# Two PSUM tiles of four banks and seven-product weights prepared a pair ahead, in a hybrid decoder layer on Trainium2

## The chip, the cores and the metric

The kernel runs on one core of one Trainium2 chip. The metric is the device time of one execution in microseconds, the median of several runs. TensorE (PE in the profile) does the matmuls, VectorE (DVE), ScalarE (ACT) and GpSimd (POOL) the rest; the SP queue issues the weight transfers.

## The reference

One layer on a sequence of 256 tokens, width 2048, float32:

```python
u = rmsnorm(h)                    # [q | k | v | z | xBC | dt | gates] = u @ w_in
A = sliding_window_sink_attention(q, k, v, sinks) @ w_attn_br
B = (rmsnorm(ssd(conv(xBC), dt) * silu(z))) @ w_ssd_br
h += (sigmoid(gate_attn) * A + sigmoid(gate_ssd) * B) @ w_o
h += (silu(rmsnorm(h) @ w_gate) * (rmsnorm(h) @ w_up)) @ w_down     # FFN 5632
h += sigmoid(rmsnorm(h) @ w_ple_gate) * (p @ w_ple_proj)
out = rmsnorm(h)
```

## The kernel before

**Products.** Every operand is split into a high part `wh` (a cast by ScalarE) and a low part `wl` (a subtraction by VectorE), and a product is three matmuls: high by high, high by low, low by high. Activations lie in SBUF transposed as such pairs (128 features by 256 tokens); weights stream from memory in transfers of 512 KB on the SP queue, through pools `wraw`, `whi`, `wlo` of 8 KB (per partition) buffers.

**Two kinds of block.** `nblock` computes 512 columns for two blocks of 128 tokens in two PSUM accumulators; the projections of the first part, attention and the SSD mixer (to about 520 us) and the per-layer embedding (from about 1480 us) use it. `wide_block` (L280) computes two column blocks by two token blocks, with the K tiles in pairs `kp`. A plain pair is 24 matmuls for each of its two halves `q`. A pair in `forms` is done with seven products in place of eight: its weights are the raw blocks b11, b21, b22 and four sums of blocks, t1 to t4 (`tr`, L328), each split again into `th` and `tl` (L336, L337), and the token side has its own sums (`token_forms`). Four of the seven go into four `shared` accumulators of the other bank group; `mid` (L352 to L355) combines these after the last formed pair, and `settle` (L360) adds them to the four main accumulators. There are 23 wide blocks (2 gates, 2 for `w_ssd_br`, 2 for `w_o`, 11 hidden, 6 for `w_down`) with 40 formed pairs; 17 of the blocks have two of them.

**PSUM.** Two pools, `acc` and `aux`, with four buffers each; every buffer is a tile of its own, one bank of 128 x 512. `psum.reverse()` swaps the groups at each wide block, so the next block's accumulators aren't those that the last block still settles.

**The side queue.** Work that isn't a product (transposes, token forms, sums of squares) waits in `side`, and `pump(n)` lets n items out between groups of matmuls. `transpose_pair` (L150) is four transposes into one bank, then `split_to`: ScalarE's cast (L132) and VectorE's subtraction (L133). For a hidden block, `settle`, ScalarE's silu (L1046) and VectorE's multiplication (L1047) come first, and two such flips of its result follow among the matmuls of the next block. In attention `p_flip` transposes the probabilities in 24 steps: two transposes (L904), a cast (L908), a subtraction (L909).

**Order.** Each engine works through its instructions in a fixed order, which the framework's scheduler makes when the kernel is built; it also places the waits, from the reads and writes of tiles.

Of the kernel before, what the change touches and what calls it, by code (L numbers as in the profile page):

```python
# [18 lines left out]
P = 128  # L19
# [4 lines left out]
NB = 512  # L24
# [37 lines left out]
def block_kernel(ctx: ExitStack, tc: tile.TileContext, x, x_t, p_t, positions, vecs, rows, g_final,  # L62
# [11 lines left out]
    acc_p = ctx.enter_context(tc.tile_pool(name="acc", bufs=4, space=bass.MemoryType.PSUM))  # L74
    aux_p = ctx.enter_context(tc.tile_pool(name="aux", bufs=4, space=bass.MemoryType.PSUM))
# [8 lines left out]
    psum = [(acc_p, "acc"), (aux_p, "aux")]  # L84

    def acc_tile():
        pool, name = psum[0]
        return pool.tile([P, NB], F32, name=name, tag=name)

    def aux_tile():  # L90
        pool, name = psum[1]
        return pool.tile([P, NB], F32, name=name, tag=name)
# [145 lines left out]
    class Sums:  # L238


        def __init__(self, tile_of, products):
            self.tile, self.left, self.first = tile_of(), 3 * products, True
# [37 lines left out]
    def wide_block(halves, lhs, nk, forms, pumps=1):  # L280
# [9 lines left out]
        c11, c12, c21, c22 = sums = [  # L290
            Sums(acc_tile, 2 * (np_ - ns) + (ns if i < 3 else 0)) for i in range(4)]
        shared, done = None, 0
        parts = [None] * 4

        def load(q, kp, dst):
            w, col0 = halves[q]
            nc.sync.dma_start(out=dst, in_=w[2 * kp * P:2 * (kp + 1) * P, col0:col0 + NB].rearrange(
                "(k p) n -> p k n", p=P))

        for kp in range(np_):  # L300
            ev, od = lhs(2 * kp), lhs(2 * kp + 1)
            tok = [[[x[:, t * P:(t + 1) * P] for x in k] for k in (ev, od)] for t in range(NT)]
            if kp not in forms:
                for q in range(2):
                    wr = wraw_p.tile([P, 2, NB], F32, name="wr", tag="wr")
                    load(q, kp, wr)
# [7 lines left out]
                    pump(pumps)  # L314
                continue
            if shared is None:
                shared = [Sums(aux_tile, ns) for _ in range(4)]
            q1, q5, q6, q7 = shared
            a, g2, f3, s3 = [[forms[kp][:, i, 0], forms[kp][:, i, 1]] for i in range(4)]
            raw = [wraw_p.tile([P, 2, NB], F32, name="wr", tag="wr") for _ in range(2)]  # L320
            for q in range(2):
                load(q, kp, raw[q])
            tr = big([P, 4, NB], F32, name="tr")
            for o, x, y in ((tr[:, 0], raw[0][:, 0], raw[1][:, 0]),
                            (tr[:, 1], raw[1][:, 0], raw[1][:, 1]),
                            (tr[:, 2], tr[:, 1], raw[0][:, 0]),
                            (tr[:, 3], tr[:, 2], raw[0][:, 1])):
                nc.vector.tensor_tensor(out=o, in0=x, in1=y, op=ALU.add)  # L328
            split = []
            for x, xh, xl in (  # L330
                    (raw[0], whi_p.tile([P, 2, NB], F32R, name="wh", tag="wh"),
                     wlo_p.tile([P, 2, NB], F32R, name="wl", tag="wl")),
                    (raw[1][:, 1:2], whi_p.tile([P, 2, NB], F32R, name="wh", tag="wh")[:, 1:2],
                     wlo_p.tile([P, 2, NB], F32R, name="wl", tag="wl")[:, 1:2]),
                    (tr, big([P, 4, NB], F32R, name="th"), big([P, 4, NB], F32R, name="tl"))):
                nc.scalar.copy(out=xh, in_=x)  # L336
                nc.vector.tensor_tensor(out=xl, in0=x, in1=xh.bitcast(F32), op=ALU.subtract)  # L337
                split.extend((xh[:, i], xl[:, i]) for i in range(x.shape[1]))
            b11, b21, b22, t1, t3, t2, t4 = split
# [3 lines left out]
            q6.add(g2, t2)  # L343
            q7.add(s3, t3)
            q5.add(a, t1)
            c21.add(tok[1][1], t4)
            pump(2 * pumps)
            done += 1
            if done == ns:
                mid = big([P, 4, NB], F32, name="mid")  # L350
                parts = [mid[:, i] for i in range(4)]
                nc.scalar.copy(out=parts[0], in_=q1.tile)  # L352
# [3 lines left out]
        return [x.tile for x in sums], parts  # L356

    def settle(i, sums, parts, out=None):
# [4 lines left out]
    def add_settled(i, dst, sums, parts):  # L363
        nc.vector.tensor_tensor(out=dst, in0=dst, in1=parts[i],
                                op=ALU.subtract if i % 2 else ALU.add)
        nc.vector.tensor_tensor(out=dst, in0=sums[i], in1=dst, op=ALU.add)
# [623 lines left out]

    gates = []
    for jj in range(2):
        sums, parts = wide_block(column_pair(w_in, GSO, jj), lhs_u, KD, uforms)
        for i in range(4):
            settle(i, sums, parts)
            nc.scalar.activation(out=parts[i], in_=parts[i], func=AF.Sigmoid,
                                 scale=r1[:, i // 2:i // 2 + 1])
        gates.append(parts)
    mforms = form_tiles((5,), "mforms")
    for jj in range(2):  # L1000
        sums, parts = wide_block(column_pair(w_ssd_br, 0, jj), lambda k: stat(yT, k), KD, yforms)
        for i in range(4):
            t, c = i // 2, cols(2 * jj + i % 2)
            settle(i, sums, parts)
            nc.vector.scalar_tensor_tensor(out=parts[i], in0=parts[i], scalar=r2[:, t:t + 1],
                                           in1=gates[jj][i], op0=ALU.mult, op1=ALU.mult)
            nc.vector.tensor_tensor(out=merged[t][:, c], in0=merged[t][:, c], in1=parts[i],
                                    op=ALU.add)
        for q in range(2):
            queue_flip(merged, mergedT, 2 * jj + q, None, mforms)  # L1010
# [14 lines left out]
    def add_to_h(jj, sums, parts):  # L1025
        for i in range(4):
            add_settled(i, h[i // 2][:, cols(2 * jj + i % 2)], sums, parts)

    ssq3 = mean_parts(4, EPS, "ssq3")
    for jj in range(2):  # L1030
        add_to_h(jj, *wide_block(column_pair(w_o, 0, jj), lambda k: stat(mergedT, k), KD, mforms))
        for q in range(2):
            queue_flip(h, hT, 2 * jj + q, V_GFFN, hforms)
            side.append(lambda j=2 * jj + q: square_sum(j, ssq3))
# [4 lines left out]
    def hidden(j, dst, kp0, forms):  # L1039
        sums, parts = wide_block(((w_gate, j * NB), (w_up, j * NB)), lambda k: stat(hT, k), KD,  # L1040
                                 hforms)
        act = [roll("act") for _ in range(NT)]
        for i in range(4):
            settle(i, sums, parts, None if i % 2 else act[i // 2])
# [12 lines left out]
    for j0, j1, apairs in thirds:  # L1057
# [13 lines left out]
        for jj in range(2):  # L1071
            add_to_h(jj, *wide_block(column_pair(w_down[j0 * NB:j1 * NB], 0, jj),
                                     lambda k, a=actT: stat(a, k), 4 * (j1 - j0), aforms))
            if last:
                for q in range(2):
                    queue_flip(h, h2T, 2 * jj + q, V_GPLE)
                    side.append(lambda j=2 * jj + q: square_sum(j, ssq4))
# [174 lines left out]
```

## Time and profile before

| | before |
|---|---|
| median of 3 runs | 1595.94 us (1594.6 to 1597.67) |
| profiled execution, its own time | 1596.97 us |
| its span, first to last instruction | 1595.3 us |
| TensorE busy | 1574.4 us, 99% |
| VectorE busy | 1200.7 us, 75% |
| ScalarE busy | 845.1 us, 53% |
| mean granted clock of TensorE | 0.997 |

Busy shares are those of the whole span. Idle time of an engine counts for the total only if it lies on the chain of work that ends last. In groups by line, the columns are busy us and mean ns of one instruction, then idle us just before them.

### The profile page before, as it was taken

The numbers are of one execution on the slowest core, as the hardware profiler recorded it, in microseconds if no ns is written. First come the engines' busy times: TensorE is split into PE (matmuls) and PEld (weight loads), VectorE is DVE, ScalarE is ACT, GpSimd is POOL, SyncE is SP. The second block draws the span as 40 slices with busy tenths as digits, with TensorE's granted clock in tenths as the row PEclk, the third lists the DMA queues.
The fourth block names the chain that finished last, engine by engine and source line by source line (L and its number), as shares of the span: only waits on it lengthen the run. The fifth ranks groups of instructions, "written<-read, shape, count | busy, mean of one in ns | idle before, by whom it ended". The sixth has DMA issues, their size and how long they took to land.

```text
span 1595.3 us, 19976 instructions
## 1 busy us (share of the span) xinstructions
PE 1574.4 (99%) x7294; PEld 1300.2 (82%) x7294; DVE 1200.7 (75%) x1507; ACT 845.1 (53%) x1073; POOL 132.1 (8%) x136
## 2 busy tenths in 40 slices
PE   9999999999999999999999999999999999999997
PEld 7988888888888888788788888788888878888886
DVE  7676767666666768788888887887877788788764
ACT  6654665555644544455655554455545444556543
POOL 1014224143210000000000000000000000000000
PEclk9999999999999999999999999999999999999999
DMA  8566435555646666665566655566665566755662
GB/s 268 175 195 183 142 105 158 159 159 158 177 158 182 210 200 212 208 195 188 175 202 191 198 193 190 185 211 194 193 195 173 196 207 195 225 188 182 197 217 100
DMA packets 152562, 296.63 MB, mean 186 GB/s; under 512 B 9536, under 2 KB 9664, under 8 KB 152080
## 3 DMA queue, kind: packets, MB, share of 16 engines
q1 hardware_dynamic: 151168, 290.76, 58.2%
q0 software_dynamic: 576, 3.47, 0.7%
q8 instruction: 57, 0.93, 0.2%
q10 hardware_dynamic: 720, 1.14, 0.2%
q14 instruction: 41, 0.34, 0.1%
HBM read 293.23 MB, written 2.10 MB: 185 GB/s over the span
## 4 chain that ended last, share of the span: by engine, by line
PE 93%; DMA 2%; DVE 2%; ACT 2%; issue 1%; POOL 0%; POOLq 0%; DVEq 0%; ACTq 0%
PE aux L248 30%; PE acc L248 27%; PE acc L204 9%; PE acc L205 9%; PE acc L206 9%; PE aux L150 1%; DMA wr<-in_w_down_dram 1%; DMA wr<-in_w_ple_gate_dram 1%; PE aux L739 1%; PE acc L150 1%; PE aux L920 1%; PE acc L233 0%; PE aux L233 0%; PE aux L234 0%; PE aux L235 0%
## 5 line engine op out<-in xcount | busy, mean ns | idle before, releaser
L308 ACT CAST wh<-wr 128x1024 fp32r<-128x1024 f32 x280 | 293.8, 1053 | 266.3 <-PE aux L248 91.6
L310 DVE TENSOR_TENSOR wl<-wr,wh 128x1024 fp32r<-128x1024 f32 x280 | 337.1, 1220 | 86.7 <-issue 37.3
L195 DVE TENSOR_TENSOR wl<-wr,wh 128x1024 fp32r<-128x1024 f32 (+1 forms) x172 | 227.6, 1330 | 122.0 <-PE acc L205 92.0
L193 ACT CAST wh<-wr 128x1024 fp32r<-128x1024 f32 (+1 forms) x172 | 173.8, 1013 | 170.9 <-PE acc L206 135.5
L248 PE MATMUL aux<-wh,flipT 128*128 128x512 f32 x736 | 237.6, 392 | 0.0
L248 PE MATMUL acc<-wh,flipT 128*128 128x512 f32 x640 | 208.3, 392 | 0.0
L204 PE MATMUL acc<-wh,uT 128*128 128x512 f32 (+1 forms) x512 | 200.2, 391 | 0.9 <-ACT cb L466 0.9
L206 PE MATMUL acc<-wh,uT 128*128 128x512 f32 (+1 forms) x512 | 194.0, 379 | 0.0
L205 PE MATMUL acc<-wl,uT 128*128 128x512 f32 (+1 forms) x512 | 193.8, 379 | 0.0
L248 PEld LDWEIGHTS aux<-wh,flipT 128*128 128x128 f32 x736 | 138.1, 188 | 28.3
L248 PE MATMUL aux<-wl,flipT 128*128 128x512 f32 x368 | 143.8, 391 | 0.5 <-DVE wl L310 0.5
L336 ACT CAST wh<-wr 128x1024 fp32r<-128x1024 f32 x80 | 66.8, 837 | 140.7 <-PE aux L248 64.0
L248 PEld LDWEIGHTS acc<-wh,flipT 128*128 128x128 f32 x640 | 120.2, 188 | 24.8 <-ACT wh L336 0.2
L248 PE MATMUL acc<-wl,flipT 128*128 128x512 f32 x320 | 124.6, 389 | 0.0
L204 PEld LDWEIGHTS acc<-wh,uT 128*128 128x128 f32 x512 | 96.3, 188 | 18.4 <-issue 1.4
L205 PEld LDWEIGHTS acc<-wl,uT 128*128 128x128 f32 x512 | 96.3, 188 | 17.6 <-issue 1.0
L337 DVE TENSOR_TENSOR tl<-tr,th 128x2048 fp32r<-128x2048 f32 x40 | 91.7, 2291 | 25.2 <-ACT th L336 25.2
L206 PEld LDWEIGHTS acc<-wh,uT 128*128 128x128 f32 x512 | 96.1, 188 | 17.8
L336 ACT CAST th<-tr 128x2048 fp32r<-128x2048 f32 x40 | 76.5, 1912 | 55.2 <-DVE tr L328 55.0
L248 PE MATMUL aux<-wh,actT 128*128 128x512 f32 x292 | 95.3, 393 | 0.0
L248 PE MATMUL acc<-wh,actT 128*128 128x512 f32 x292 | 93.5, 390 | 0.0
L328 DVE TENSOR_TENSOR tr<-wr 128x512 f32<-128x512 f32 x80 | 52.8, 686 | 40.3 <-DMA wr<-in_w_down_dram 21.7
(476 smaller groups left out, 2764.5 us busy)
## 6 DMA issues: line engine op xcount, KB each, us to landing
wr<-in_w_in_dram SPq DMA_DIRECT2D x144, 512.0 KB, 3.7
wr<-in_w_gate_dram SPq DMA_DIRECT2D x88, 512.0 KB, 3.8
wr<-in_w_up_dram SPq DMA_DIRECT2D x88, 512.0 KB, 4.4
wr<-in_w_down_dram SPq DMA_DIRECT2D x88, 512.0 KB, 4.4
wr<-in_w_ssd_br_dram SPq DMA_DIRECT2D x32, 512.0 KB, 4.8
wr<-in_w_o_dram SPq DMA_DIRECT2D x32, 512.0 KB, 4.2
wr<-in_w_ple_gate_dram SPq DMA_DIRECT2D x32, 512.0 KB, 4.6
wr<-in_w_in_dram SPq DMA_DIRECT2D x32, 256.0 KB, 4.2
```

The costliest lines, as they stand in the source:

```text
L150: nc.tensor.transpose(out=ps[:, j, t * P:(t + 1) * P], in_=src[t][:, c:c + P], identity=ident)
L193: nc.scalar.copy(out=wh, in_=wr)
L195: nc.vector.tensor_tensor(out=wl, in0=wr, in1=wh.bitcast(F32), op=ALU.subtract)
L204: nc.tensor.matmul(o, hi[:, ts], wh[:, kk, cs], start=(k == 0), stop=False)
L205: nc.tensor.matmul(o, hi[:, ts], wl[:, kk, cs], start=False, stop=False)
L206: nc.tensor.matmul(o, lo[:, ts], wh[:, kk, cs], start=False, stop=(k == nk - 1))
L248: nc.tensor.matmul(self.tile, a, b, start=self.first, stop=self.left == 0)
L308: nc.scalar.copy(out=wh, in_=wr)
L310: nc.vector.tensor_tensor(out=wl, in0=wr, in1=wh.bitcast(F32), op=ALU.subtract)
L328: nc.vector.tensor_tensor(out=o, in0=x, in1=y, op=ALU.add)
L336: nc.scalar.copy(out=xh, in_=x)
L337: nc.vector.tensor_tensor(out=xl, in0=x, in1=xh.bitcast(F32), op=ALU.subtract)
```

## The change

PSUM becomes two tiles of four banks (`Banks`, a ring of four through `take`), so that one VectorE operation can cover two banks: settling is 2 operations of 2 x 512 per block in place of 4 of 512, `mid` takes 3 VectorE operations in place of 4, and what follows (gates, merge, the addition to h) goes over 1024 columns. A formed pair's raw weights lie in one 8 KB tile `raw` and are prepared by the generator `prepared` in three steps beside the pair in front: the two transfers; the sums (one operation of 1024, two of 512) and the casts; the subtractions. Nothing is pumped while `shared` is in use, and otherwise `pump(min(2 * kp + q, 2))`; the sums of squares of h are queued behind both flips. Matmuls and transposes are as many as before. The diff, cut:

```diff
-    acc_p = ctx.enter_context(tc.tile_pool(name="acc", bufs=4, space=bass.MemoryType.PSUM))
-    aux_p = ctx.enter_context(tc.tile_pool(name="aux", bufs=4, space=bass.MemoryType.PSUM))
+    psum_p = ctx.enter_context(tc.tile_pool(name="psum", bufs=1, space=bass.MemoryType.PSUM))
+    class Banks:
+        def __init__(self, name):
+            self.all, self.next, self.held = psum_p.tile([P, 4, NB], F32, name=name), 0, False
+        def take(self):
+            assert not self.held
+            self.next = (self.next + 1) % 4
+            return self.all[:, (self.next - 1) % 4]
+    psum = [Banks("acc"), Banks("aux")]
...
-    def wide_block(halves, lhs, nk, forms, pumps=1):
+    def wide_block(halves, lhs, nk, forms):
...
-        c11, c12, c21, c22 = sums = [
-            Sums(acc_tile, 2 * (np_ - ns) + (ns if i < 3 else 0)) for i in range(4)]
+        mine, other = psum
+        c11, c12, c21, c22 = [
+            Sums(mine.all[:, i], 2 * (np_ - ns) + (ns if i < 3 else 0)) for i in range(4)]
...
+        def prepared(kp):
+            raw = big([P, 4, NB], F32, name="raw")
+            nc.sync.dma_start(out=raw[:, 0:4:3], in_=block(1, kp))
+            nc.sync.dma_start(out=raw[:, 1:3], in_=block(0, kp))
+            yield
+            tr = big([P, 4, NB], F32, name="tr")
+            th = big([P, 4, NB], F32R, name="th")
+            nc.vector.tensor_tensor(out=tr[:, 0:2], in0=raw[:, 1:4:2],
+                                    in1=raw[:, 0:1].broadcast_to([P, 2, NB]), op=ALU.add)
+            for i in (2, 3):
+                nc.vector.tensor_tensor(out=tr[:, i], in0=tr[:, i - 1], in1=raw[:, i - 1],
+                                        op=ALU.add)
+            wh = [whi_p.tile([P, 2, NB], F32R, name="wh", tag="wh") for _ in range(2)]
+            nc.scalar.copy(out=wh[0], in_=raw[:, 1:3])
+            nc.scalar.copy(out=wh[1][:, 0], in_=raw[:, 3])
+            nc.scalar.copy(out=th, in_=tr)
+            yield
+            wl = [wlo_p.tile([P, 2, NB], F32R, name="wl", tag="wl") for _ in range(2)]
+            tl = big([P, 4, NB], F32R, name="tl")
+            for x, xh, xl in ((raw[:, 1:3], wh[0], wl[0]), (raw[:, 3], wh[1][:, 0], wl[1][:, 0]),
+                              (tr, th, tl)):
+                nc.vector.tensor_tensor(out=xl, in0=x, in1=xh.bitcast(F32), op=ALU.subtract)
+            yield
...
             if kp not in forms:
+                step(kp + 1)
                 for q in range(2):
...
-                    pump(pumps)
+                    step(kp + 1)
+                    if shared is None or mid is not None:
+                        pump(min(2 * kp + q, 2))
                 continue
             if shared is None:
-                shared = [Sums(aux_tile, ns) for _ in range(4)]
+                shared = [Sums(other.all[:, i], ns) for i in range(4)]
+                other.held = True
...
-            pump(2 * pumps)
...
-                for o, x, y, op in ((3, 0, q6, ALU.subtract), (2, 3, q7, ALU.add),
-                                    (1, 3, q5, ALU.add), (3, 2, q5, ALU.add)):
-                    nc.vector.tensor_tensor(out=parts[o], in0=parts[x], in1=y.tile, op=op)
...
+                nc.vector.tensor_tensor(out=mid[:, 3], in0=mid[:, 0], in1=q6.tile,
+                                        op=ALU.subtract)
+                nc.vector.tensor_tensor(out=mid[:, 1:3],
+                                        in0=mid[:, 3:4].broadcast_to([P, 2, NB]),
+                                        in1=other.all[:, 1:3], op=ALU.add)
+                nc.vector.tensor_tensor(out=mid[:, 3], in0=mid[:, 2], in1=q5.tile, op=ALU.add)
+                other.held = False
...
-        nc.vector.tensor_tensor(out=parts[i] if out is None else out, in0=sums[i], in1=parts[i],
-                                op=ALU.subtract if i % 2 else ALU.add)
...
+        for i, op in enumerate((ALU.add, ALU.subtract)):
+            nc.vector.tensor_tensor(out=mid[:, i:4:2], in0=mine.all[:, i:4:2], in1=mid[:, i:4:2],
+                                    op=op)
+        return mid
```

How the order moves. First TensorE's order at a hidden block's join, around the second flip of the finished hidden block (`act<-` or `mid<-` is what is transposed, `flipT` the tokens of the block that runs). A wait is named by its semaphore: DVE_49 is VectorE's, Activation_49 ScalarE's. Before:

```order
3230 L248 MATMUL acc<-wl,flipT 128x512
3231 L248 MATMUL acc<-wh,flipT 128x512
3232 L150 MATMUL aux<-ident,act 128x128 x4
3233 L248 MATMUL acc<-wh,flipT 128x512 [waits Activation_49]
3234 L248 MATMUL acc<-wl,flipT 128x512
3235 L248 MATMUL acc<-wh,flipT 128x512 x2
3236 L248 MATMUL acc<-wl,flipT 128x512
3237 L248 MATMUL acc<-wh,flipT 128x512 x2
3238 L248 MATMUL acc<-wl,flipT 128x512
```

And of the change at the same place (L157 are the transposes, L255 the products):

```order
3227 L255 MATMUL acc<-wl,flipT 128x512
3228 L255 MATMUL acc<-wh,flipT 128x512
3229 L157 MATMUL aux<-ident,mid 128x128 [waits DVE_49]
3230 L157 MATMUL aux<-ident,mid 128x128 x3
3231 L255 MATMUL aux<-wh,flipT 128x512 [waits DVE_49,Activation_49]
3232 L255 MATMUL acc<-wh,flipT 128x512 [waits Activation_49]
3233 L255 MATMUL acc<-wl,flipT 128x512 [waits DVE_49]
3234 L255 MATMUL acc<-wh,flipT 128x512 x2
3235 L255 MATMUL acc<-wl,flipT 128x512
```

The transposes and the two matmuls behind them now stand behind waits for VectorE and ScalarE, and one of the matmuls writes into the group that the flip uses (`aux`). ScalarE's order there, before (L132 is the flip's cast, L308 and L336 weight casts):

```order
517 L1046 ACTIVATE act<-act,r_6432 128x512 [waits Pool_49]
518 L1046 ACTIVATE act<-act,r_6432 128x512 [waits DVE_49]
519 L308 CAST wh<-wr 128x1024 [waits DMAHW4_49,PE_49,Activation_49]
520 L336 CAST wh<-wr 128x1024 [waits DMAHW5_49,PE_49,Activation_49]
521 L132 CAST actT<-aux 128x512 [waits PE_49]
522 L336 CAST wh<-wr 128x512 [waits DMAHW6_49,PE_49,Activation_49]
523 L132 CAST actT<-aux 128x512 [waits PE_49]
524 L308 CAST wh<-wr 128x1024 [waits DMAHW7_49,DVE_49,PE_49]
525 L336 CAST th<-tr 128x2048 [waits DVE_49]
526 L308 CAST wh<-wr 128x1024 [waits DMAHW0_49,PE_49,Activation_49]
```

And of the change (L139 is the flip's cast, L321 to L323 cast a formed pair's weights, L351 a plain pair's):

```order
536 L1069 ACTIVATE mid<-mid,r_6160 128x512 [waits Pool_49]
537 L1069 ACTIVATE mid<-mid,r_6160 128x512
538 L139 CAST actT<-aux 128x512 [waits DVE_49,PE_49] x2
539 L321 CAST wh<-raw 128x1024 [waits DMAHW1_49]
540 L322 CAST wh<-raw 128x512 [waits DMAHW0_49,Activation_49]
541 L351 CAST wh<-wr 128x1024 [waits DMAHW4_49,Activation_49]
542 L351 CAST wh<-wr 128x1024 [waits DMAHW5_49,Activation_49]
543 L323 CAST th<-tr 128x2048 [waits DVE_49]
```

The two flips' casts stand side by side now, and three weight casts follow them that stood partly ahead of them. Last, TensorE's order at the probability flips (L904 before, L927 in the change). Before:

```order
883 L904 MATMUL aux<-ident,sc 128x128 [waits DVE_49,Pool_49]
884 L904 MATMUL aux<-ident,sc 128x128
885 L204 MATMUL acc<-wh,uT 128x512 [waits Activation_49]
886 L904 MATMUL aux<-ident,sc 128x128 [waits DVE_49,Pool_49]
887 L904 MATMUL aux<-ident,sc 128x128
888 L904 MATMUL aux<-ident,sc 128x128 [waits Activation_49]
889 L904 MATMUL aux<-ident,sc 128x128
890 L205 MATMUL acc<-wl,uT 128x512
891 L904 MATMUL aux<-ident,sc 128x128 [waits Activation_49]
892 L904 MATMUL aux<-ident,sc 128x128
893 L206 MATMUL acc<-wh,uT 128x512
894 L204 MATMUL acc<-wh,uT 128x512
```

And of the change:

```order
924 L927 MATMUL aux<-ident,sc 128x128 [waits DVE_49,Pool_49]
925 L927 MATMUL aux<-ident,sc 128x128
926 L927 MATMUL aux<-ident,sc 128x128 [waits DVE_49]
927 L927 MATMUL aux<-ident,sc 128x128
928 L927 MATMUL aux<-ident,sc 128x128 [waits DVE_49]
929 L927 MATMUL aux<-ident,sc 128x128
930 L927 MATMUL aux<-ident,sc 128x128 [waits DVE_49]
931 L927 MATMUL aux<-ident,sc 128x128
932 L927 MATMUL aux<-ident,sc 128x128 [waits DVE_49]
933 L927 MATMUL aux<-ident,sc 128x128
```

Projection matmuls (L204 to L206) stood between the pairs of transposes; now five pairs follow one another, each behind a wait for VectorE.

## Rows read from the trace of the kernel before

**Rows 1.** The page: span, busy time of the engines, the chain by engine.
```profile
span 1595.3 us, 19976 instructions
...
PE 1574.4 (99%) x7294; PEld 1300.2 (82%) x7294; DVE 1200.7 (75%) x1507; ACT 845.1 (53%) x1073; POOL 132.1 (8%) x136
...
PE 93%; DMA 2%; DVE 2%; ACT 2%; issue 1%; POOL 0%; POOLq 0%; DVEq 0%; ACTq 0%
```

**Rows 2.** Windows by stage: length, busy us (instructions) of PE, PEld, DVE, ACT, POOL; clock; DMA.
```profile
0.00:520.00 520.00, 515.07 (x2519) 430.47 (x2520) 357.19 (x527) 294.84 (x444) 125.92 (x128) 1.00 0.58 171
520.00:1480.00 960.00, 954.42 (x4264) 781.59 (x4263) 770.97 (x889) 494.36 (x547) 3.88 (x5) 1.00 0.61 196
1480.00:1596.00 116.00, 104.94 (x514) 88.10 (x512) 72.55 (x93) 55.94 (x82) 2.30 (x3) 0.97 0.50 165
```

**Rows 3.** What TensorE waited for: us in total, times, longest.
```profile
PE acc L248 <- DVE wl L337: 3.6, 3, 1.5
...
PE acc L204 <- ACT cb L466: 0.9, 1, 0.9
```

**Rows 4.** The chain of waits, one step in a wide block: start, us.
```profile
662.55 11.56 PE acc L248 x51
```

**Rows 5.** Timeline of a hidden block's join: start, us, engine, line.
```profile
814.75 0.60 PE L150 MATMUL aux<-ident,act 128*128 128x128 f32 x4
...
815.10 0.48 PE L248 MATMUL acc<-wh,flipT 128*128 128x512 f32 x1
...
815.51 0.58 ACT L132 CAST actT<-aux 128x512 fp32r<-128x512 f32 x1
...
816.13 0.69 DVE L133 TENSOR_TENSOR actT<-aux,actT 128x512 fp32r<-128x512 f32 x1
```

**Rows 6.** Groups by line, wide blocks: busy, mean ns of one; idle before.
```profile
L337 DVE TENSOR_TENSOR tl<-tr,th 128x2048 fp32r<-128x2048 f32 x40 | 91.7, 2291 | 25.2 <-ACT th L336 25.2
...
L336 ACT CAST th<-tr 128x2048 fp32r<-128x2048 f32 x40 | 76.5, 1912 | 55.2 <-DVE tr L328 55.0
...
L328 DVE TENSOR_TENSOR tr<-tr,wr 128x512 f32<-128x512 f32 x80 | 55.1, 688 | 1.6
...
L337 DVE TENSOR_TENSOR wl<-wr,wh 128x1024 fp32r<-128x1024 f32 x40 | 48.8, 1219 | 2.0 <-PE aux L248 1.1 <-issue 0.9
...
L336 ACT CAST wh<-wr 128x1024 fp32r<-128x1024 f32 x40 | 42.2, 1054 | 90.8 <-PE aux L248 42.6 <-PE acc L248 34.7 <-DMA wr<-in_w_down_dram 11.6
...
L336 ACT CAST wh<-wr 128x512 fp32r<-128x512 f32 x40 | 24.8, 620 | 49.9 <-PE aux L248 21.4 <-PE acc L248 20.6 <-DVE wl L337 5.9
...
L1046 ACT ACTIVATE act<-act,r 128x512 f32<-128x512 f32 x22 | 15.8, 722 | 1.0
...
L1047 DVE SCALAR_TENSOR_TENSOR act<-mid,r,act 128x512 f32<-128x512 f32 x22 | 15.5, 746 | 0.0
...
L275 DVE TENSOR_TENSOR fm<-fsc 128x128 f32<-128x128 f32 x22 | 5.7, 285 | 1.8 <-ACT fsc L255 1.8
```

**Rows 7.** Groups by line, first part: probability flips, an evacuation, a table load.
```profile
L909 DVE TENSOR_TENSOR pt<-aux,pt 128x256 fp32r<-128x256 f32 x24 | 8.8, 417 | 1.0 <-ACT pt L908 0.9
...
L904 PE MATMUL aux<-ident,sc 128*128 128x128 f32 x48 | 8.2, 279 | 0.8 <-DVE pt L909 0.7
...
L908 ACT CAST pt<-aux 128x256 fp32r<-128x256 f32 x24 | 7.9, 380 | 1.3 <-PE aux L904 1.0
...
L466 ACT ACTIVATE xs<-acc,r 128x512 f32<-128x512 f32 x8 | 5.3, 688 | 0.3 <-PE acc L206 0.3
...
L520 ACT ACT_TABLE_LOAD x3 | 3.8, 1283 | 0.1
```

**Rows 8.** Windows of the first 12 us, the same columns as rows 2.
```profile
0.00:7.00 7.00, 3.77 (x16) 3.36 (x16) 2.71 (x13) 4.19 (x9) 4.80 (x49) 1.00 0.74 253
...
8.50:10.00 1.50, 1.50 (x5) 1.22 (x4) 0.96 (x1) 0.79 (x2) 0.00 (x0) 0.50 0.70 261
10.00:12.00 2.00, 2.00 (x7) 1.53 (x7) 1.19 (x4) 0.70 (x3) 0.00 (x0) 0.62 1.05 398
```

More of the change, by code (lines that the diff above doesn't have):

```diff
@@ L238, in block_kernel, with __init__ @@
     class Sums:
-        def __init__(self, tile_of, products):
-            self.tile, self.left, self.first = tile_of(), 3 * products, True
+        def __init__(self, tile, products):
+            self.tile, self.left, self.first = tile, 3 * products, True
         def add(self, lhs, rhs):
@@ L278, in token_forms, with block, step @@
                                 op=ALU.subtract)
-    def wide_block(halves, lhs, nk, forms, pumps=1):
+    def wide_block(halves, lhs, nk, forms):
         psum.reverse()
         np_, ns = nk // 2, len(forms)
-        c11, c12, c21, c22 = sums = [
-            Sums(acc_tile, 2 * (np_ - ns) + (ns if i < 3 else 0)) for i in range(4)]
-        shared, done = None, 0
-        parts = [None] * 4
-        def load(q, kp, dst):
-            w, col0 = halves[q]
-            nc.sync.dma_start(out=dst, in_=w[2 * kp * P:2 * (kp + 1) * P, col0:col0 + NB].rearrange(
-                "(k p) n -> p k n", p=P))
+        mine, other = psum
+        c11, c12, c21, c22 = [
+            Sums(mine.all[:, i], 2 * (np_ - ns) + (ns if i < 3 else 0)) for i in range(4)]
+        sums = [c11, c12, c21, c22]
+        shared, done, mid = None, 0, None
+        def block(q, kp):
+            w, col0 = halves[q]
+            return w[2 * kp * P:2 * (kp + 1) * P, col0:col0 + NB].rearrange("(k p) n -> p k n", p=P)
+        def prepared(kp):
[21 more added lines that the diff above has]
+            yield
+            yield ([(wh[i // 2][:, i % 2], wl[i // 2][:, i % 2]) for i in range(3)]
+                   + [(th[:, i], tl[:, i]) for i in range(4)])
+        ready = {}
+        def step(kp):
+            if kp in forms:
+                if kp not in ready:
+                    ready[kp] = prepared(kp)
+                return next(ready[kp])
@@ L313, in wide_block @@
                             sums[2 * t + q].add(tok[t][k], (wh[:, k], wl[:, k]))
-                    pump(pumps)
+                    step(kp + 1)
+                    if shared is None or mid is not None:
+                        pump(min(2 * kp + q, 2))
                 continue
             if shared is None:
-                shared = [Sums(aux_tile, ns) for _ in range(4)]
-            q1, q5, q6, q7 = shared
+                shared = [Sums(other.all[:, i], ns) for i in range(4)]
+                other.held = True
+            q1, q5, q7, q6 = shared
             a, g2, f3, s3 = [[forms[kp][:, i, 0], forms[kp][:, i, 1]] for i in range(4)]
[L320 to L339, printed above, removed]
+            b11, b21, b22, t1, t2, t3, t4 = step(kp)
             q1.add(tok[0][0], b11)
@@ L1039, in hidden @@
     def hidden(j, dst, kp0, forms):
[L1040 to L1044, printed above, removed]
+        sums = wide_block(((w_gate, j * NB), (w_up, j * NB)), lambda k: stat(hT, k), KD, hforms)
+        act = [sums[:, 2 * t] for t in range(NT)]
         for t in range(NT):
             nc.scalar.activation(out=act[t], in_=act[t], func=AF.Silu, scale=r3[:, t:t + 1])
[L1047 removed]
+            nc.vector.scalar_tensor_tensor(out=act[t], in0=sums[:, 2 * t + 1],
                                            scalar=r3[:, t:t + 1], in1=act[t], op0=ALU.mult,
@@ L1076, in block_kernel @@
                     queue_flip(h, h2T, 2 * jj + q, V_GPLE)
+                for q in range(2):
                     side.append(lambda j=2 * jj + q: square_sum(j, ssq4))
```

63 lines of the change are left out of this document (27 added, 36 removed).

## The prediction

> **What bounds the kernel now.** I read the page first, then the stages, the waits of TensorE, the chain that ended last, and the durations of single operations. TensorE is busy for 1574.4 of 1595.3 us and 93% of the chain that ended last is its own work [rows 1]: the time is the matmuls one behind another, and anything that opens a gap between two of them costs its full length. By stages [rows 2] TensorE stood still for 520.00 - 515.07 = 4.9 us in the first part (projections, attention, SSD), for 5.6 us in the middle part (the 23 wide blocks) and for 11.1 us in the last. The waits say the same: the longest entry is 3.6 us in three waits for a weight's low part [rows 3]. A step of the chain shows the unit I count in: 51 matmuls of a wide block in 11.56 us, 0.227 us each [rows 4]. So nearly nothing is left to win, at most the 5.6 us in the blocks that the change rewrites, and what matters is whether it opens gaps.
>
> **What it removes.** A formed pair's sums go from four VectorE operations of 0.69 to one of 1.22 and two of 0.69 [rows 6], mid and the settling shrink in the same way, about 130 operations in all. VectorE is busy 80% of the middle part [rows 2] and TensorE doesn't wait for its throughput: worth nothing by itself. Preparing a formed pair's weights beside the pair in front can take away the weight waits of the wide blocks: I credit all 5.6 us, and 1 us of the first part, so **-6.6 us** (bounds 0 and -10.5, all idle time of the two parts). The transfers of `raw` start a pair earlier (48 matmuls x 0.227 = 10.9 us), cover enough; if the 8 KB buffer came free late, they would hold the loads queued behind them on SP, which I bound at 0.5 us for each of 40 pairs, 20 us, and take at nothing. Matmuls stay as many. The settling now starts at a block's end, not while its last matmuls run: for a hidden block 1.22 + 2 x 0.72 + 0.75 = 3.4 us [rows 6] up to the transposes, and the 24 matmuls ahead of them last 5.4 us, so it is covered.
>
> **What it adds: waits, by the order of the built kernel.** Four banks are now one tile, and the built program guards the tile, not the bank: a write to any of its banks waits until every earlier reader of any other has finished. In the rows of the order, the second flip's transposes carry a wait for VectorE that they didn't have, and the first matmul of the formed pair is placed right behind them with a wait for VectorE and ScalarE. What is between a matmul and the TensorE instruction that its wait hangs on is one to three instructions there; before it was seven at least.
>
> Before, the same place ran like this [rows 5]: transposes from 814.75 to 815.35, ScalarE's cast from 815.51 to 816.09, VectorE's subtraction to 816.82, and TensorE went on with matmuls into other banks from 815.10. The hand-overs took 0.16 and 0.04 us.
>
> (A) The hidden joins. Count from the end of the second flip's transposes: cast at 0.16, done at 0.74; then ScalarE has to make, in its order, the first high part (1.05, to 1.79), the second (0.62, to 2.41) and the next block's (1.05, to 3.46). VectorE finishes the flip's low part at 0.74 + 0.04 + 0.69 = 1.47, then the sums, 1.22 + 0.69 + 0.69 (to 4.07), then the low part for which the third matmul waits, 1.22 (to 5.29) [rows 6]. TensorE has two matmuls of 0.227 meanwhile: a hole of **4.8 us**. Of the 11 hidden blocks six have it so, and two also make token forms there (four VectorE operations of 0.285 [rows 6]), 6.0 us: 6 x 4.8 + 2 x 6.0 = **41 us**. If only the flip was waited for, it would be 1.47 us each, 12 us: the lower bound; the upper is 48, 6.0 us for all eight.
> (B) The join from w_o to the first hidden block is the same with a gain in its flips: 6.4 us (1.5 to 8).
> (C) Elsewhere a flip has 8 to 12 matmuls (1.8 to 2.7 us) behind it before its tile is used again, against 1.47 us and one or two weight casts of 1.05 in front: 0.3 to 0.9 us at 13 places, 6.7 us (0 to 12).
> (D) In the 17 blocks with two formed pairs, the second pair's th and tl (1.91 and 2.29 [rows 6]) stand ahead of the low part of the block beside it: 0.35 us each, 6 us (0 to 15).
> (E) The 11 joins of projection blocks in the first part: the next block's first matmul waits for both evacuations of the last one, on one engine 2 x 0.69 [rows 7], some of it on two engines at once. Before it waited for neither, but for one stall of 0.9 us [rows 3]. I take 13.5 us (0.5 each: 5.5; 2.0 each: 22).
> (F) Attention and SSD: a step of the probability flips is two transposes, a cast and a subtraction, 0.28 + 0.38 + 0.42 [rows 7] plus hand-overs of 0.2, which used to run beside projection matmuls and the other three banks. The order has five in a row with no matmul between. The 24 steps and the decay products come to 14.3 us, 4.0 of it behind a table load of 1.28 [rows 7] and an evacuation; the query flips, the key flip and the rest to 19 us: 33.4 (20 to 45).
> (G) The last part: four joins of the per-layer embedding blocks at about 2.8 and 3.5 us, two ScalarE activations and their VectorE work, of the size of the first part's 0.69 [rows 7]: 11.7 us (6 to 16).
>
> Sum of the gaps 41 + 6.4 + 6.7 + 6 + 13.5 + 33.4 + 11.7 = **119 us** (45 to 166).
>
> **The clock.** After the first 7 us, in which TensorE was busy for 3.77, it ran at a granted clock of 0.50 from 8.50 to 10.00 (1.2 in place of 2.4 GHz) [rows 8], and the mean clock of the last part, the one with idle time, is 0.97 against 1.00 in the others [rows 2]. A hole of 5 us may do the same. A stretch as long as that one costs 0.75 us of work at least, 1.5 with the next slow stretch; I take 1.5 us at four of the holes, **6 us** (0 to 27, at 18 places).
>
> The profiled execution took 1596.97 us, 0.06% above the median of 1595.94. 1596.97 + 119 - 6.6 + 6 = **1715 us**.
>
> **Rivals.** *The cross-bank waits cost nothing* (the one on the other side: faster). If they are all met when TensorE comes to them, only the weight waits go: 1597 - 6.6 = 1590 us, at best 1586.5. For it: before, TensorE wrote one group of banks while ScalarE and VectorE read another, and was never held [rows 5]. The Trainium skill ("PSUM — Partial Sum Buffer", section "PSUM bank collisions raise a hardware error") asks to guard PSUM by bank and quadrant, and says that accesses to different banks run clean side by side; guarded like that, the change would be this rival, 1590 us. The rows of before agree with the rule, but the change's program guards more than it asks. Against it: the waits are in the built order, and at A the time between is 0.45 us against 5.3. It decides from the point where the gaps sum to less than 6.6 us, a twentieth of what I count: 0.03.
> *About half of the gaps.* Engines that run ahead of TensorE, and matmuls that I count as following but that fill, leave about 60 us: 1597 + 60 - 6.6 = 1650 us (1625 to 1680). For it: D and C are small differences of large numbers; E and F rest on many short chains. 0.15.
> *The clock falls at every hole.* 1597 + 119 - 6.6 + 27 = 1736, with the upper ends of E and F up to 1775. For it: rows 8. Against: TensorE is never idle for 5 us in the middle of the trace of before, so no row shows one. 0.15.
> *It does nothing that can be measured*, gains and gaps cancelling: 1594 to 1600: 0.02.
>
> **How the numbers follow.** The forecast (1680 to 1750) has 0.65. The range 1645 to 1765 holds it, over half of the half-gap case and most of the clock case. What a measurement of this kernel can tell from no change is about 0.2%, 3.2 us. Faster 0.03, same 0.02, slower 0.95.
>
> **What would show it.** In the profile after: TensorE's busy time about the same (1575 to 1590) in a longer span, share near 92%; waits of TensorE on a formed pair's first matmuls for a low part on VectorE, eight times near 5 us; waits of the projection blocks' first matmul for the evacuation, 11 times; the probability flips in steps of about 1.2 us; the middle part longer by about 55 us. It is wrong if the matmuls behind the second flip start within 1 us of the transposes, or if the wide part isn't longer.

## The result: slower by 12.8%, 204 us

The changed kernel takes 1799.28 us (median of 4 runs, 1798.19 to 1802.17), the kernel before 1595.49 us beside it: a ratio of 1.1279, 95% interval 1.1266 to 1.1293. I had forecast 1715 us, with a range up to 1765: the direction was right and the size was not. The profiled execution took 1799.43 us. The page, in the lines that answer to [rows 1], and the clock by 40 slices of the span in tenths:

```profile
span 1797.7 us, 19804 instructions
...
PE 1655.4 (92%) x7294; PEld 1331.2 (74%) x7294; DVE 1202.2 (67%) x1374; ACT 846.3 (47%) x1069; POOL 124.0 (7%) x136
...
PEclk9999969999999999999999999999999999999998
```

TensorE has as many instructions as before (7294), but is busy 1655.4 - 1574.4 = 81.0 us longer, and idle 142.3 us in place of 20.9. These two numbers are the whole difference of the spans: 121.4 us of gaps and 81.0 us of more busy time for the same matmuls, 202.4 us. The clock's line points at the larger cause of the second: the mean granted clock is 0.956 in place of 0.997.

The stages begin and end here at the first and the last product of a wide block. Before (columns as in [rows 2]):

```profile
0.00:500.00 500.00, 495.07 (x2431) 413.90 (x2432) 342.32 (x512) 285.12 (x435) 125.92 (x128) 1.00 0.58 171
500.00:1483.60 983.60, 978.02 (x4368) 801.16 (x4367) 789.43 (x910) 505.14 (x557) 3.88 (x5) 1.00 0.61 196
1483.60:1596.00 112.40, 101.34 (x498) 85.11 (x497) 68.95 (x87) 54.89 (x81) 2.30 (x3) 0.97 0.50 164
```

After:

```profile
0.00:584.30 584.30, 526.19 (x2430) 421.58 (x2431) 349.05 (x515) 288.77 (x436) 118.25 (x128) 0.95 0.50 148
584.30:1666.70 1082.40, 1021.73 (x4368) 821.06 (x4367) 781.14 (x771) 502.44 (x552) 3.40 (x5) 0.96 0.54 177
1666.70:1798.00 131.30, 107.52 (x498) 88.57 (x497) 71.99 (x88) 55.05 (x81) 2.30 (x3) 0.93 0.43 140
```

| | idle of TensorE, before | after | growth | forecast | busy of TensorE, growth |
|---|---|---|---|---|---|
| first part | 4.9 us | 58.1 us | +53.2 | +45.9 (E, F, less 1) | +31.1 |
| wide blocks | 5.6 | 60.7 | +55.1 | +54.5 (A to D, less 5.6) | +43.7 |
| last part | 10.4 | 23.5 | +13.1 | +11.7 (G) | +6.2 |

(The last windows reach 0.7 and 0.3 us past the span, which is taken off.)

So the gaps are in the stages where the prediction put them and of its size, 121 us in place of 112. What it missed is the last column.

What TensorE waited for, the columns as in [rows 3]. L255 are the products of the wide blocks, L927 the probability flips' transposes, L211 the first matmul of a projection, L1190 one of the last part:

```profile
PE acc L255 <- DVE wl L353: 16.0, 13, 1.8
PE acc L255 <- ACT wh L321: 9.1, 4, 3.0
...
PE aux L927 <- DVE pt L932: 8.1, 8, 2.1
...
PE acc L211 <- DVE merged L996: 6.5, 2, 4.0
...
PE acc L211 <- ACT sz L543: 5.0, 2, 3.7
...
PE acc L1190 <- ACT gt L1115: 4.6, 1, 4.6
```

And the join of [rows 5] in the changed kernel, in time (start, us, engine, line; in brackets the idle time before and what ended it):

```profile
920.70 0.60 PE L157 MATMUL aux<-ident,mid 128*128 128x128 f32 x4
921.34 0.58 ACT L139 CAST actT<-aux 128x512 fp32r<-128x512 f32 x1 [2.14 <-PE aux L157]
921.82 1.05 ACT L321 CAST wh<-raw 128x1024 fp32r<-128x1024 f32 x1
921.96 0.69 DVE L140 TENSOR_TENSOR actT<-aux,actT 128x512 fp32r<-128x512 f32 x1 [2.03 <-ACT actT L139]
922.56 1.22 DVE L315 TENSOR_TENSOR tr<-raw 128x1024 f32<-128x1024 f32 x1
922.76 0.62 ACT L322 CAST wh<-raw 128x512 fp32r<-128x512 f32 x1
...
922.92 0.50 PE L255 MATMUL aux<-wh,flipT 128*128 128x512 f32 x1 [1.62 <-ACT wh L321]
923.28 1.99 ACT L351 CAST wh<-wr 128x1024 fp32r<-128x1024 f32 x2
923.81 1.42 DVE L318 TENSOR_TENSOR tr<-tr,raw 128x512 f32<-128x512 f32 x2
...
924.38 0.49 PE L255 MATMUL acc<-wh,flipT 128*128 128x512 f32 x1 [0.96 <-ACT wh L351]
925.15 1.22 DVE L353 TENSOR_TENSOR wl<-wr,wh 128x1024 fp32r<-128x1024 f32 x1
...
926.42 0.71 PE L255 MATMUL acc<-wl,flipT 128*128 128x512 f32 x1 [1.54 <-DVE wl L353]
```

The transposes end at 921.30. ScalarE has waited 2.14 us for them; then come the flip's cast, the formed pair's (L321, L322), the running pair's (L351); VectorE does the low part, the sums and at last the low part that TensorE's third matmul waits for, at 926.42. Between there are two matmuls. I had worked out 5.29 us from the transposes' end to that matmul; it took 5.12.

### The profile page after: what moved, and what is told of

Read it like the earlier page. It is cut to its first block, busy times and chain, and to the rows that moved or that the text cites. A ratio compares the mean times of both kernels' runs of the same rounds, so it can differ in the third digit from the quotient of the medians.

```text
span 1797.7 us, 19804 instructions
## 1 busy us (share of the span) xinstructions
PE 1655.4 (92%) x7294; PEld 1331.2 (74%) x7294; DVE 1202.2 (67%) x1374; ACT 846.3 (47%) x1069; POOL 124.0 (7%) x136
## 4 chain that ended last, share of the span: by engine, by line
PE 50%; DVE 7%; DMA 5%; issue 4%; ACT 2%; SPq 0%; POOL 0%; POOLq 0%; DVEq 0%; ACTq 0%
PE aux L255 22%; PE acc L255 22%; DVE wl L353 3%; DMA raw<-in_w_down_dram 2%; PE acc L211 1%; PE acc L212 1%; PE acc L213 1%; DVE tr L315 1%; DVE tr L318 1%; DMA raw<-in_w_gate_dram 1%; DMA raw<-in_w_o_dram 1%; DVE h L1052 1%; DVE mid L387 1%; DMA wr<-in_w_ple_gate_dram 1%; DMA raw<-in_w_ssd_br_dram 1%
## 5 line engine op out<-in xcount | busy, mean ns | idle before, releaser
L351 ACT CAST wh<-wr 128x1024 fp32r<-128x1024 f32 x280 | 291.4, 1053 | 334.6 <-PE aux L255 154.2
L255 PE MATMUL aux<-wh,flipT 128*128 128x512 f32 x736 | 243.0, 401 | 10.9 <-ACT wh L321 8.3
L255 PE MATMUL acc<-wh,flipT 128*128 128x512 f32 x640 | 217.2, 408 | 13.4 <-ACT wh L321 7.7
L211 PE MATMUL acc<-wh,uT 128*128 128x512 f32 (+1 forms) x512 | 203.3, 397 | 12.7 <-ACT sz L543 5.0
L212 PE MATMUL acc<-wl,uT 128*128 128x512 f32 (+1 forms) x512 | 199.8, 390 | 0.9 <-DVE wl L202 0.9
L213 PE MATMUL acc<-wh,uT 128*128 128x512 f32 (+1 forms) x512 | 198.0, 387 | 0.0
L255 PEld LDWEIGHTS aux<-wh,flipT 128*128 128x128 f32 x736 | 142.2, 193 | 43.3 <-ACT wh L321 10.0
L255 PEld LDWEIGHTS acc<-wh,flipT 128*128 128x128 f32 x640 | 125.9, 197 | 42.2 <-ACT wh L321 8.4
L255 PE MATMUL aux<-wl,flipT 128*128 128x512 f32 x368 | 148.9, 405 | 5.7 <-DVE wl L353 5.1
L255 PE MATMUL acc<-wl,flipT 128*128 128x512 f32 x320 | 131.5, 411 | 8.3 <-DVE wl L353 7.6
L211 PEld LDWEIGHTS acc<-wh,uT 128*128 128x128 f32 x512 | 98.5, 192 | 33.5 <-ACT sz L543 5.8
L255 PE MATMUL aux<-wh,actT 128*128 128x512 f32 x292 | 97.4, 401 | 1.6 <-ACT wh L351 1.6
L255 PE MATMUL acc<-wh,actT 128*128 128x512 f32 x292 | 96.1, 400 | 1.4 <-ACT wh L321 1.4
L255 PEld LDWEIGHTS aux<-wl,flipT 128*128 128x128 f32 x368 | 71.6, 195 | 25.8 <-DVE wl L353 11.1
L323 ACT CAST th<-tr 128x2048 fp32r<-128x2048 f32 x40 | 76.2, 1906 | 20.4 <-DVE tr L318 20.1
L255 PEld LDWEIGHTS acc<-wl,flipT 128*128 128x128 f32 x320 | 63.0, 197 | 25.8 <-DVE wl L353 12.9
```

The source lines that it names most:

```text
L211: nc.tensor.matmul(o, hi[:, ts], wh[:, kk, cs], start=(k == 0), stop=False)
L212: nc.tensor.matmul(o, hi[:, ts], wl[:, kk, cs], start=False, stop=False)
L213: nc.tensor.matmul(o, lo[:, ts], wh[:, kk, cs], start=False, stop=(k == nk - 1))
L255: nc.tensor.matmul(self.tile, a, b, start=self.first, stop=self.left == 0)
L323: nc.scalar.copy(out=th, in_=tr)
L351: nc.scalar.copy(out=wh, in_=wr)
```

## The experiments

Ten kernels. The first four ask whether the guard of four banks as one tile is the cause, and what the clock is worth.

**A tile for each bank.**

```diff
-            self.all, self.next, self.held = psum_p.tile([P, 4, NB], F32, name=name), 0, False
+            self.tiles = [psum_p.tile([P, NB], F32, name=f"{name}{i}") for i in range(4)]
+            self.next, self.held = 0, False
...
-                nc.vector.tensor_tensor(out=mid[:, 1:3],
-                                        in0=mid[:, 3:4].broadcast_to([P, 2, NB]),
-                                        in1=other.all[:, 1:3], op=ALU.add)
+                for i in (1, 2):
+                    nc.vector.tensor_tensor(out=mid[:, i], in0=mid[:, 3], in1=other.tiles[i],
+                                            op=ALU.add)
```

> The changed kernel with a PSUM tile for each bank (eight tiles) in place of two tiles of four; the VectorE operations across two banks become two of one bank each; the preparation of formed pairs beside the pair in front and the new rule of pumping stay. Theory (waits come from guarding four banks as one tile): the gaps of TensorE go, TensorE idle falls from 142 us to under 35 us, the granted clock is back to 0.99 or more, time 1580 to 1610 us. Rival (the early preparation or the new pumping order makes the gaps): TensorE still idle for over 90 us, time over 1700 us.

Measured: 1661.45 us, ratio 1.0409 (1.0394 to 1.0425), clock 0.982, idle of TensorE 56.6 us. Neither theory nor rival: 138 us of the loss are gone, 66 us stay. By stages the first part takes 500.0 us and the last 110.6 (500.0 and 111.7 before); the wide blocks take 1050.1 us in place of 983.7, and of 1082.4 in the changed kernel. So the guard made all of the loss outside the wide blocks and 32 us of it inside, and something else is left there. The same join in this kernel shows what:

```profile
829.66 0.60 PE L158 MATMUL aux<-ident,mid 128*128 128x128 f32 x4
830.29 0.59 ACT L140 CAST actT<-aux 128x512 fp32r<-128x512 f32 x1 [2.59 <-PE aux L158]
830.77 1.05 ACT L322 CAST wh<-raw 128x1024 fp32r<-128x1024 f32 x1
...
832.24 1.99 ACT L352 CAST wh<-wr 128x1024 fp32r<-128x1024 f32 x2
...
834.10 1.22 DVE L354 TENSOR_TENSOR wl<-wr,wh 128x1024 fp32r<-128x1024 f32 x1
...
835.37 0.79 PE L256 MATMUL acc<-wl,flipT 128*128 128x512 f32 x1 [1.04 <-DVE wl L354]
```

Transposes to 830.26, and the low part's matmul at 835.37, 5.1 us later, with no tile in common between the flip and the running pair's sums. What is left is the order of ScalarE and VectorE, argued from these lines and tested by e5 to e8 below: the running pair's weights (L352, L354) stand behind the flip's cast (L140), which waited 2.59 us for the transposes, and behind the formed pair's cast (L322) and sums, whose products come after the running pair's in the program.

**The four-bank tiles alone**, in the kernel before:

```diff
-    psum = [(acc_p, "acc"), (aux_p, "aux")]
+    psum = [Banks("acc"), Banks("aux")]
...
-                    pump(pumps)
+                    if shared is None or done == ns:
+                        pump(pumps)
...
-            pump(2 * pumps)
...
+                pump(2 * pumps)
```

> The kernel before with only its PSUM pools replaced by two tiles of four banks; preparation and VectorE operations as before (side work isn't let out while the shared accumulators are in use, since a ring of banks needs that). Theory: most of the loss is there without the rest of the change, 1730 to 1830 us, idle of TensorE over 90 us, clock under 0.97. Rival (the preparation makes the gaps): under 1640 us.

Measured: 1745.51 us, ratio 1.0931 (1.0914 to 1.0947), clock 0.971, idle 123.9 us. As the theory has it, but for the clock, which is just above its bound of 0.97: +150 us, of which the first part has 581.6 - 500.0 = 81.6, the wide blocks 51 and the last part 16. TensorE's waits in the wide blocks (L253) are for other weights here, the formed pair's sums; the flips (L910) are as in the changed kernel:

```profile
PE acc L253 <- ACT th L342: 17.3, 3, 6.0
...
PE aux L910 <- DVE pt L915: 8.1, 8, 2.1
```

**Tiles of two banks**, so that VectorE still works across two:

```diff
+            self.pairs = [psum_p.tile([P, 2, NB], F32, name=f"{name}{i}") for i in range(2)]
...
+        def bank(self, i):
+            return self.pairs[i % 2][:, i // 2]
```

> The changed kernel with four PSUM tiles of two banks, paired so that VectorE still works across two banks at once; consecutive takes go to different tiles. Theory (a wait is met when the guarded group is smaller, and the next flip uses the other tile): between the two, nearer to the bank tiles: 1600 to 1670 us, the hidden joins' holes of 4.8 us gone. Rival (any tile over more than one bank loses as much): over 1740 us.

Measured: 1700.59 us, ratio 1.0656 (1.0638 to 1.0673): between theory and rival, and the hidden joins' holes are not gone. The first part is 516.2 us, so 16 of 84 us are left of what the guard did there. The wide blocks take 1062.7 us, nearly what they take with a tile for each bank: as e1 shows, their holes don't need the guard, and that's what I had got wrong in the expectation.

**The holes filled**, in the changed kernel:

```diff
+                    while fill:
+                        for i in range(fill.pop()):
+                            nc.tensor.matmul(sums[i % 4].tile, zero, wh[:, 0], start=False,
+                                             stop=False)
...
+        if j + 1 not in (4, 8, 11):
+            side[-1] = lambda run=side[-1]: (run(), fill.append(20))
```

> The changed kernel with 20 matmuls by a tile of zeros added into the open accumulators (the sums stay the same) behind the second flip's transposes at the eight joins from a hidden block to a hidden block: 20 x 0.227 = 4.5 us of TensorE work in a hole of 4.8 us. Theory (the clock's fall behind a hole costs as much as I left out): the hole stays as long but the clock stays at 1.00 behind it, 2 to 3.5 us less for each of eight, 1770 to 1785 us, mean clock 0.965 to 0.975. Rival (the extra 81 us of TensorE busy time comes from something other than the clock, say from slower matmuls while other engines use the same tile): time the same or longer, 1795 to 1815 us.

Measured: 1781.3 us, ratio 1.1161 (1.1134 to 1.1188), mean clock 0.970, as the theory has it: 18 us less, with 160 matmuls more. One join and what follows it, in the changed kernel:

```profile
1010.00:1021.00 11.00, 11.00 (x52) 9.14 (x51) 6.82 (x7) 2.98 (x4) 0.00 (x0) 1.00 0.75 238
1021.00:1026.00 5.00, 2.42 (x10) 1.31 (x9) 2.93 (x4) 3.62 (x5) 0.00 (x0) 0.95 0.00 0
1026.00:1032.00 6.00, 4.70 (x12) 3.57 (x12) 5.35 (x5) 2.21 (x2) 0.00 (x0) 0.50 0.60 192
```

And with the hole filled:

```profile
1010.00:1021.00 11.00, 11.00 (x52) 9.12 (x51) 6.82 (x7) 2.98 (x4) 0.00 (x0) 1.00 0.74 237
1021.00:1027.00 6.00, 6.00 (x29) 4.92 (x29) 3.94 (x5) 3.69 (x5) 0.00 (x0) 1.00 0.01 3
1027.00:1032.00 5.00, 4.93 (x22) 3.77 (x21) 5.00 (x5) 3.80 (x4) 0.00 (x0) 1.00 0.68 222
```

In the changed kernel TensorE was busy for 2.42 of 5.00 us and then ran 6 us at a granted clock of 0.50 (1.2 in place of 2.4 GHz). With the hole filled it stays at 1.00. The page of the filled kernel:

```profile
span 1785.5 us, 20118 instructions
...
PE 1673.6 (94%) x7454; PEld 1349.6 (76%) x7454; DVE 1201.9 (67%) x1375; ACT 847.9 (47%) x1069; POOL 124.0 (7%) x136
```

1673.6 us less 160 x 0.227 of zeros is 1637.3, 18.1 us less than the changed kernel's 1655.4: **2.3 us of slow matmuls for each of the eight holes**, shown by taking them away. In the changed kernel TensorE was busy for 41.01 us in the eight stretches at a granted clock of 0.50 behind these joins, where matmuls in a row start 0.427 us apart and not 0.227; 41.01 x (1 - 0.227 / 0.427) = 19.2 us, 2.4 for each, agrees. The profiled execution of the filled kernel is the slowest of its four (1787.18 us): its idle time is only 30.4 us shorter with 36.3 us of zeros, so its span is shorter by 12.2 us.

The next four ask what the 66 us in e1 are, and whether they are the changed kernel's too.

**Preparation behind the second half**, with a tile for each bank:

```diff
-                    step(kp + 1)
+                    if q:
+                        step(kp + 1)
+                        step(kp + 1)
```

> The kernel of e1 (a PSUM tile for each bank) with steps two and three of a formed pair's preparation let out behind the second half of the pair in front, not behind its first and second. Theory (in e1 the 66 us left come from ScalarE's order: the weights of the pair in front's second half are cast behind the two flips' casts and the formed pair's): that cast now stands ahead of the flips' casts, the holes behind the second flip go, TensorE idle under 30 us, 1590 to 1605 us. Rival (something else of the new wide block is late, such as the rule of letting out no side work while the shared accumulators are in use, or settling at the block's end): 1640 to 1660 us.

Measured: 1619.53 us, ratio 1.0146 (1.0131 to 1.0161), clock 0.997, idle 32.5 us. Between theory and rival: 42 of the 66 us are gone and 24 are left. In the join where a flip also makes token forms, ScalarE still stands for 2.59 us before the flip's cast (L140), and the formed pair's cast (L322) behind it is late, though TensorE waits for it for 0.26 us only; the waits that are left in the wide blocks are short ones like it, the longest 2.1 us:

```profile
865.24 0.59 ACT L140 CAST actT<-acc 128x512 fp32r<-128x512 f32 x1 [2.59 <-PE acc L158]
...
867.13 1.05 ACT L322 CAST wh<-raw 128x1024 fp32r<-128x1024 f32 x1
...
868.23 0.50 PE L256 MATMUL acc<-wh,flipT 128*128 128x512 f32 x1 [0.26 <-ACT wh L322]
```

**Side work let out as before**, one piece a half, and **preparation at the pair itself**, each with a tile for each bank:

```diff
-                        pump(min(2 * kp + q, 2))
+                        pump(1)
```

```diff
-                step(kp + 1)
...
-                    step(kp + 1)
...
+            for _ in range(3):
+                step(kp)
```

> The kernel of e1 with one piece of side work let out behind each half, as before, in place of min(2 kp + q, 2). Theory as in e5 (ScalarE's order at the join): in the built order the second half's cast stands ahead of the flips here too, so 1590 to 1615 us. Rival (the early steps alone do it, wherever the flips stand): 1640 to 1660 us.

> The kernel of e1 with all steps of the preparation at the formed pair itself, as before. Theory as in e5: 1590 to 1610 us. Rival (the preparation isn't what the 66 us come from): 1640 us or more.

Measured: 1629.8 us, ratio 1.0208 (1.0191 to 1.0226), and 1622.39 us, 1.0166 (1.0151 to 1.0182). Alone they take off 32 and 39 us, between theory and rival: neither the early steps nor the late flips make the 66 us by themselves.

**Preparation behind the second half in the changed kernel**, with its two tiles of four banks (the edit of e5):

> The changed kernel (two tiles of four banks) with the same late steps as e5. Theory (the holes at the hidden joins come from ScalarE's order and not, as I predicted, from guarding four banks as one tile): some 60 us less than the changed kernel, 1725 to 1750 us. Rival (the tile's guard makes these holes by itself): 1780 to 1800 us.

Measured: 1798.34 us, ratio 1.1267 (1.1249 to 1.1286), the same as the changed kernel, as the rival has it. The holes have only moved on, from the running pair's weights to the formed pair's sums, which were no entry above 1.7 us in the changed kernel:

```profile
PE aux L255 <- ACT th L323: 11.9, 6, 2.2
PE aux L255 <- DVE tl L329: 11.8, 7, 2.3
PE acc L255 <- DVE tl L329: 10.8, 8, 1.9
```

With the guard the order's fault can't be mended by this edit; without it 42 us come back.

The last two close the sum.

**Late steps and side work as before, a tile for each bank** (the edits of e5 and e6 together; the steps still stand beside the pair in front):

> The kernel of e5 (a PSUM tile for each bank, preparation behind the second half) with one piece of side work let out behind each half, as before. Theory (the 24 us that e5 still loses come from the flips, which stand one and two halves later than before and hold ScalarE's queue while it waits for their transposes): 1595 to 1605 us, TensorE idle about 21 us as before. Rival (they come from what e5, e6 and e7 share: no side work while the shared accumulators are in use, and raw weights in the buffers of 8 KB): 1612 to 1630 us.

Measured: 1601.51 us, ratio 1.0032 (1.002 to 1.0044), clock 0.997. As the theory has it: letting the flips out as before takes off 18 of the 24 us; the 5.8 us that are left I didn't follow further.

**The control of e2**, with its ring and held side work, a tile for each bank:

> The kernel of e2 with eight fixed PSUM tiles of one bank, in a ring, in place of two of four banks: so the kernel before with a ring and no side work let out while the shared accumulators are in use. Theory (the guard of four banks alone made e2 150 us slower): within 0.5% of the kernel before, 1590 to 1604 us. Rival (the ring, or holding side work back, costs by itself): 1612 us or more.

Measured: 1595.09 us, ratio 1.0003 (0.9994 to 1.0012). The ring and the held side work cost nothing, so the 150 us of e2 are the guard's.

| median us | a tile for each bank | two tiles of four banks |
|---|---|---|
| old preparation and pumping | 1595.09 (e10) | 1745.51 (e2) |
| the change's | 1661.45 (e1) | 1799.28 (the change) |
| the change's, steps late | 1619.53 (e5) | 1798.34 (e9) |
| steps late, old pumping | 1601.51 (e8) | not run |

150 and 66 us alone, 204 together. None of these is faster than the kernel before: with TensorE busy 99% of the span there was nothing to win, as far as these kernels show.

## Why the prediction was wrong in size, point by point

- **What bounds the kernel**: right. TensorE's own time and its gaps make the whole of both spans, and no gain showed anywhere.
- **The sum of gaps, 119 - 6.6 = 112 us**: right, 121.4 us by the trace, and stage by stage as in the table above. Inside the wide blocks that is in part luck: the eight hidden joins left TensorE idle for 32.4 us where (A) had 41, the join from w_o for 4.9 where (B) had 6.4, and the rest of the wide blocks for 23.4 where (C) and (D) had 12.7.
- **(A), the hidden joins, 4.8 us each**: the path was of the forecast's length (5.12 us from the transposes to the matmul, where I had 5.29; TensorE was idle for 4.12 of them, as each of the two matmuls between took 0.50 and not 0.227), the cause only in part. The arithmetic ran through ScalarE's and VectorE's order, but I put the hole down to the guard of four banks. e1 shows the same hole without the guard, so the order was enough for it. With the guard the one other order of the steps that was tried (e9) has holes behind other weights and gains nothing.
- **(E), (F), (G), joins of projections, flips, the last part**: the guard is the cause, shown by e1 (both parts back to 500.0 and 110.6 us) and e2 with e10. The flips run in steps as forecast, 1.61 us from one pair of transposes to the next here, where I had 1.28. The 0.28 that I took for two transposes is the mean of one [rows 7]; two took 0.41 at full clock and 0.69 at half clock:

```profile
228.15 0.41 PE L927 MATMUL aux<-ident,sc 128*128 128x128 f32 x2 [0.36 <-DVE pt L932]
...
230.50 0.69 PE L927 MATMUL aux<-ident,sc 128*128 128x128 f32 x2 [1.93 <-DVE pt L932]
231.22 0.37 ACT L931 CAST pt<-aux 128x256 fp32r<-128x256 f32 x1 [2.03 <-PE aux L927]
231.63 0.42 DVE L932 TENSOR_TENSOR pt<-aux,pt 128x256 fp32r<-128x256 f32 x1 [1.19 <-ACT pt L931]
...
232.11 0.69 PE L927 MATMUL aux<-ident,sc 128*128 128x128 f32 x2 [0.92 <-DVE pt L932]
```

- **The clock, 6 us (0 to 27)**: this is the step that failed. Busy time grew by 81.0 us, which is three times its upper end. The larger part is the clock. In the changed kernel's span there are 27 stretches at a granted clock of 0.50; the kernel before has two, one in its first 12 us and one behind its last matmul. Here are the longest stretch, where the probability flips follow one another and beyond, and the sum of all 27, in the columns of [rows 2]:

```profile
230.22:257.53 27.31, 16.46 (x45) 10.81 (x46) 5.80 (x13) 6.83 (x12) 2.37 (x1) 0.50 0.07 19
...
sum 157.79, PE 120.68 PEld 89.77 DVE 98.49 ACT 55.40 POOL 12.83; mean PE 4.47 PEld 3.32 DVE 3.65 ACT 2.05 POOL 0.48
```

TensorE was busy for 120.68 us at half clock, where it was 3.4 before. Matmuls in a row start 0.427 us apart there (the median, counted in the trace; the two below are such a pair) and not 0.227 [rows 4]:

```profile
842.20 0.63 PE L255 MATMUL acc<-wl,flipT 128*128 128x512 f32 x1
842.63 1.06 PE L255 MATMUL acc<-wh,flipT 128*128 128x512 f32 x2
```

So the clock cost (120.68 - 3.4) x (1 - 0.227 / 0.427) = 55 us. I had let it fall at four holes at 1.5 us each, the price of [rows 8]; it fell in 25 places where it didn't before, at 2.2 us on average, and behind the eight hidden joins at each. And I had asked what single holes cost: the stretch from 230 to 257 costs 7.7 us, in a part of the program that I had counted only as gaps. (The mean clock, 0.956 over 1797.7 us, gives 79 us, but that counts idle time in the slow stretches too; that it is near 81 is chance. And the 0.97 of the last part in [rows 2], which I took for a sign, was no loss: from 1588.50 on, at 0.50, TensorE had no matmul.)

The other 26 us of busy time I had put at nothing. Matmuls in a row come 0.227 us apart [rows 4], but one that stands alone between two waits counts with its whole time: the two in the hole of the join above, at a granted clock of 1.00, took 0.50 us each.

```profile
922.00:926.40 4.40, 1.00 (x2) 0.37 (x2) 4.33 (x6) 4.40 (x5) 0.00 (x0) 1.00 0.00 0
```

Counted in the traces, TensorE's work falls into 112 pieces without a break in place of 15. An estimate from these numbers, 97 x (0.50 - 0.227) = 26 us, agrees; e1 has 46 pieces, so 8.5 us by the same estimate, where its busy time leaves 8.6 beside the clock. No experiment tests this part by itself. Together the forecast missed 9 us of gaps, 49 us of clock and 26 us of matmuls that stand alone: 84 us.

- **The rivals**: the third, a clock that falls at every hole, is the nearest to what happened. I gave it 0.15 and 1736 us; with the upper ends of E and F that is 1756, not the 1775 that I wrote, and either is short of 1799, as its 27 us for the clock were 55. The clock didn't fall at every hole: there are 89 of over 0.3 us, and 25 slow stretches. The first (waits that cost nothing) and the second (half of the gaps) are out. The Trainium skill ("PSUM — Partial Sum Buffer", section "PSUM bank collisions raise a hardware error") gives bank and quadrant, or simply the bank, as the unit to guard PSUM by. It states no time; here a guard by bank cost nothing by itself (e10, 1595.09 us). But the change with a guard by bank took 1661.45 us (e1), not the 1590 that I gave for it, since the order made holes of its own.
- **What would show it**: the span's share of TensorE at 92%, as said, and the eight hidden joins had their holes, each as three waits (1.62, 0.96 and 1.54 us in the join above) and not as one near 5 us. The matmuls behind the flip started 1.62 us after the transposes. The middle part is longer by 98.8 us, not 55, and "busy time about the same (1575 to 1590)" is the line that came out wrong; both are the same mistake.

## What to carry to other kernels

A tile that spans several PSUM banks was guarded as one here: before widening an operation of an engine with time to spare, look in the built order at what now waits behind every reader of every bank. A gap on the engine that bounds a kernel costs its length, then the slow matmuls behind it, and the matmuls that stand alone in it, so price all three, and price a chain of short gaps as one slow stretch. And take the parts of a change apart: here the order made holes without the guard, and mending the order with the guard in place showed nothing (e9).

## What the runs showed of the hardware

A hole of some 5 us in TensorE's work, with two matmuls in it, was followed by 6 us at a granted clock of 0.50, and 4.5 us of matmuls by zeros in the same hole kept the clock at 1.00. Work that contributes nothing to the result made the kernel 18 us faster, with 36 us more of it. And a matmul that stood alone at a granted clock of 1.00 kept TensorE busy for 0.50 us, where one in a row takes 0.227.
